# Token sums of two pairs in one set of instructions, 198 pairs by seven products, the last half store on ScalarE's queue, and the first two k tiles in loads of 512 KB

## The chip, the cores and the metric

The kernel runs on one core of a Trainium2 chip (trn2). The metric is the device time of one execution in microseconds (us); a verdict compares medians of several executions of both kernels on the same chip. An instruction belongs to TensorE (PE, with its weight loads PEld), VectorE (DVE), ScalarE (ACT), GpSimd (POOL) or SyncE (SP). SP, POOL and ACT also issue DMA transfers, each through a queue of its own.

## The reference

One layer of a decoder on 256 tokens and 2048 features, in f32, in which nearly all the work is products of the tokens with weight matrices:

```python
h = rmsnorm(x, g_mix[i])
proj = h @ w_in[i]
x_r, g_r, q, k, v, gate_r, gate_a = jnp.split(proj, IN_SPLIT_POINTS, axis=-1)
...
y_r = jax.nn.gelu(g_r) * rg_lru(xc, w_rg_a[i], b_rg_a[i], w_rg_x[i], b_rg_x[i], lru_lambda[i])
y_r = y_r @ w_rnn_out[i]
...
y_a = o.transpose(0, 2, 1, 3).reshape(B, S, D_ATTN) @ w_attn_out[i]
mix = jax.nn.sigmoid(gate_r) * y_r + jax.nn.sigmoid(gate_a) * y_a
x = x + mix @ w_o[i]
h = rmsnorm(x, g_ffn[i])
gu = h @ w_ffn_gu[i]
g, u = jnp.split(gu, 2, axis=-1)
x = x + (jax.nn.silu(g) * u) @ w_ffn_down[i]
ple_gate = jax.nn.sigmoid(rmsnorm(x, g_ple[i]) @ w_ple_gate[i])
x = x + ple_gate * (p[i] @ w_ple_proj[i])
```

## The kernel before

Every f32 operand is split into two parts that TensorE takes in the type float32r: a high part (ACT copies the values into that type) and a low part (DVE subtracts the high part from the values). A product is then three matmuls, high by high, high by low and low by high; `prod` issues them, 128 x 128 of tokens by 128 x 512 of weights each. Names: `raw` and `r` are weights as loaded, `whi`/`wlo` and `shi`/`slo` their parts, `xg`, `hg`, `act`, `mix`, `y`, `ost`, `h3` the split tokens, and `xs`, `hgs`, `as`, `ms`, `ys`, `os`, `h3s` split sums of tokens.

`group` computes the two token tiles (t = 0, 1) by two blocks of 512 columns (A and B), over all k tiles of 128 features. Two k tiles are a pair, and a pair is taken in one of two ways. Plain, it is eight products. By seven products it is a scheme of Strassen's kind over the 2 x 2 token blocks and 2 x 2 weight blocks of the pair: seven products, of which four use sums of weights and four sums of tokens. Two pairs by seven always go together; their weights lie in one tile of 128 x 1024, so that each of the items "11", "21", "22", "T1", "T2", "T3", "T4" is one high part on ACT, one low part on DVE and two products. For T1 to T4 the weights must first be summed: by a DMA of POOL that adds from HBM onto the tile (`pr.add`), or by a `tensor_tensor` of DVE (names `r<-r,r`), which for T1 and T3 needs the block 12 loaded as well (`r12`). The table `how` of `CFG` says, for each group, which of them POOL adds; `xr`, `gu` and the other lists of `CFG` say which pairs go by seven.

The token sums of a pair come from `half_sums`: its 128 x 512 of tokens are four blocks; one DVE instruction of 256 columns and two of 128 make four sums, and `split` makes their high part on ACT and their low part on DVE, 512 columns each.

The first product "T1" of a group is stored in a PSUM bank, from which ACT copies it into a second one ("seeds"), since both blocks need it; the next products that go into the first bank wait for that copy. The copies of PSUM banks by ACT are written `q<-q`, `u<-q`, `pair<-q`, `pair<-u`.

After a group, its results are scaled and gated on ACT and DVE and then turned by TensorE (`pr.turns`, names `gut`, `hgt`, `mxt`, `h3t`, four matmuls of 128 x 128 a pair), before they are the tokens of later groups. These steps are hooks of the group that follows, at the items that `turn` lists.

The order on each engine is no code order: `make` builds all operations, and `schedule` places them by due times with a cost table, under 54 tiles of 128 x 1024 and 8 PSUM banks; `improve` repeats that. So a change of a table moves instructions everywhere. Within an engine and within a queue, order is fixed: an instruction that waits holds back all behind it.

At the start, nine matmuls on zeros (`warm`) keep TensorE busy, and the first k tiles are loaded one by one, 256 KB for each block. At the end, `embed` (`pp`) and the gate give the last output tiles, which SP stores; the last one is stored in two halves.

Of the kernel before, what the change touches and what calls it, by code (L numbers as in the profile page):

```python
# [11 lines left out]
P = 128  # L12
# [79 lines left out]
class Program:  # L92
# [95 lines left out]
    def store(self, dst, i, kb, name="", writes=(), cap=None):  # L188
        return self.op("SP", 0.06, 0.0, lambda nc: nc.sync.dma_start(dst(nc), i.ap()), [i], list(writes), size=kb,
                       name=name, cap=cap)  # L190
# [397 lines left out]
def order_of(ks, nd, lead=0):  # L588
# [24 lines left out]
def build(cfg):  # L613
# [100 lines left out]
    def half_sums(h, name):  # L714


        q = tile("hs", "H")
        a11, a12 = h[:P], h[2 * P:3 * P]
        s3, s1, s2, s4 = (q[c * P:c * P + P] for c in range(4))
        pr.vec(2 * P, lambda nc: nc.vector.tensor_tensor(  # L720
            R3(2)(q[:2 * P].ap()), R3(2)(h[:2 * P].ap()), R3(3)(h[P:].ap())[:, ::2, :], ALU.subtract),
               [h.all], [q[:2 * P]], name="hs")
        tt(s2, s1, a11, ALU.subtract, name="hs")
        tt(s4, a12, s2, ALU.add, name="hs")
        t = split(q.all, name)
        return [(t[c * P:c * P + P], t[512 + c * P:640 + c * P]) for c in (1, 2, 0, 3)]
# [30 lines left out]
    def group(w, cols, ks, pairs, sums, tokens, how, hooks=None, lead=0):  # L757
# [7 lines left out]
        early = {x for x in order if x[0] in "AB"} if lead and nd else ()  # L765
# [13 lines left out]
        for n, x in enumerate(order):  # L779
# [3 lines left out]
            m, dp = x[:2]  # L783
            if m in ("A", "B"):
# [98 lines left out]
    def x_sums(ps):  # L883
        for p in ps:
            if p not in xsum:
                h = tile("h", "H")
                tt(h.all, xg[p][:512].f32(), xg[p][512:].f32(), ALU.add, name="h")
                xsum[p] = half_sums(h, "xs")

    x_sums(xp)  # L890
    for b in range(4):
        for t in range(2):
            q = tile("xq", "H")
            pr.load(q.all, dram("x", (lambda t, b: lambda a: a[t * P:t * P + P, b * 512:b * 512 + 512])(t, b)), 256,
                    name="xq", early=None)
            squares(0, t, b, q.all)
# [34 lines left out]
    xc, xcs, y, ysum, hr = {}, {}, [], {}, {}  # L931

# [54 lines left out]
    def finish(p):  # L987
# [4 lines left out]
        tt(r.all, ps.all, r.all, ALU.mult, name="y")  # L992
        y.append(split(r.all, "y"))
        if p in union("ro"):
            ysum[p] = half_sums(r, "ys")
# [114 lines left out]
    heads, osum = {}, {}  # L1110
    qs, ks_, zst, ost = {}, {}, {}, []
# [95 lines left out]
    def att_o(hp):  # L1207
# [18 lines left out]
        if hp in union("ao"):  # L1226
            h = tile("h", "H")
            act(h.all, ps.all, AF.Copy, name="h")
            ost.append(split(h.all, "ost"))
            osum[hp] = half_sums(h, "os")  # L1230
        else:
            ost.append(split(ps.all, "ost"))
# [54 lines left out]
    mix, msum = {}, {}  # L1287

    def next_mix(p):
        def run():  # L1290
# [6 lines left out]
            if p in union("wo"):  # L1297
                h = tile("h", "H")
                act(h.all, ps.all, AF.Copy, name="h")
                mix[p] = split(h.all, "mix")  # L1300
                msum[p] = half_sums(h, "ms")
# [32 lines left out]
    def next_h(hs, sums, p, gcol, pairs, name):  # L1334
        def run():
            ps = turned(p, name + "t")
            g = pc(gcol, 2 * p, 2)
            if p in pairs:
                h = tile("h", "H")
# [3 lines left out]
                hs[p] = split(h.all, name)  # L1343
                sums[p] = half_sums(h, name + "s")
# [4 lines left out]
    hg, hsum = {}, {}  # L1349
    for g in range(2):  # L1350
# [11 lines left out]
        for p in range(4 * g, 4 * g + 4):  # L1362
            pend.append(next_h(hg, hsum, p, PC_GF, union("gu"), "hg"))
# [4 lines left out]
    h3, sum3 = {}, {}  # L1368
    q_of = [q for q in range(len(FQ)) for _ in range(FQ[q])]
    f0 = [sum(FQ[:q]) for q in range(len(FQ))]  # L1370
    dn_pairs = {p for v in cfg["dn"] for u in v for p in u}

    def gu(g):
# [13 lines left out]
        def turn(f):  # L1387
            def run():
# [4 lines left out]
                if p in dn_pairs:  # L1393
                    h = tile("h", "H")
                    act(h.all, ps.all, AF.Copy, name="h")
                    acts[p] = split(h.all, "act")
                    asum[p] = half_sums(h, "as")
# [6 lines left out]
    def down(q, g):  # L1404
# [19 lines left out]
        if q == len(FQ) - 1:  # L1424
            for p in range(4 * g, 4 * g + 4):
                pend.append(next_h(h3, sum3, p, PC_GP, union("pg"), "h3"))
# [22 lines left out]
    for g in range(2):  # L1449
# [7 lines left out]
        for n in (0, 2, 3, 1) if g else range(4):  # L1457
# [7 lines left out]
            for s in cut:  # L1465
# [3 lines left out]
                    t, 1024 * g + 512 * b, s)), d[s], (s.stop - s.start) // 2, name="out")  # L1469
# [7 lines left out]
CFG = dict(xr=[X2, X2, X4, X4, X4], ro=[F6, F4], gtr=[X4] * 2, v=[X6, X8], qk=[X4, X6, X4, X4], gta=[X4] * 2,  # L1477
           ao=[F4] * 2, wo=[F4, F6], gu=[F4, X8, *[F6] * 9], pg=[F4, X8], dn=[[F4, F6], [[8, 9, 10, 11]] * 2,
           [[16, 17, 18, 19]] * 2], how=dict(xr=[NONE, LATER, SOON, TWO, SOON], gtr=[SOON, ONE], v=[TWO] * 2,
           qk=[SOON, TWO, TWO, ONE], gta=[ALL, LATER], ro=[TWO, ALL], ao=[TWO, SOON], wo=[TWO] * 2, gu=[TWO,  # L1480
           SOON, TWO, LATER, TWO, TWO, TWO, LATER, TWO, TWO, LATER], pg=[ALL, TWO], dn=[ONE, NONE, TWO]),
           lead=8, order=('g1', 'r0', 'r1'), att0=4, every=9, at=(0, 4, 10, 16), turn=[3, 5, 7, 9])
# [5 lines left out]
def make():  # L1488
    pr = build(CFG)
# [79 lines left out]
```

## Time and profile before

| what | value |
|---|---|
| median of 3 runs | 1794.31 us (1792.18 to 1794.45) |
| the profiled execution | 1792.39 us, span 1790.7 us in the profile |
| DMA | 440.54 MB, mean 246 GB/s |
| slowest issue to landing | weights added by POOL, 215 of 512 KB, 8.7 us in the median |
| granted TensorE clock | 0.999 |

A row of the timeline reads: start in us from the span's start, length in us, engine, source line, operation, written tile <- read tiles, sizes, count; in brackets the idle time of the engine before it and what ended that. Lengths of neighbours overlap, so what an instruction costs its engine in a full row is the distance from its start to the next one's.

### The profile page before, as it was taken

How to read it: one execution, taken by the hardware profiler on the slowest of the kernel's cores; microseconds unless marked ns; L12 is line 12 of the kernel's file. 1: busy time of each engine (PE TensorE's matmuls, PEld its weight loads, DVE VectorE, ACT ScalarE, POOL GpSimd, SP SyncE). 2: the span in 40 equal slices, each digit the busy share in tenths (PEclk: the TensorE clock that was granted, in tenths of full speed). 3: DMA queues.
4: the chain of work that ended last, by engine and by line, in shares of the span. 5: the costliest groups of instructions: out<-in, count | busy, mean ns of one | idle time of the engine just before them, and what ended most of it. 6: DMA issues, size and time to landing. Idle time of an engine off the chain costs nothing.

```text
span 1790.7 us, 23886 instructions
## 1 busy us (share of the span) xinstructions
PE 1779.9 (99%) x8295; PEld 1483.2 (83%) x8295; DVE 1675.0 (94%) x1933; ACT 1423.0 (79%) x1962; POOL 202.6 (11%) x239
## 2 busy tenths in 40 slices
PE   9999999999999999999999999999999999999998
PEld 7888888888888888888888888888888788888887
DVE  8999887998799899899999999999999898999989
ACT  8999999876567799999777878677677666778875
POOL 0000000011011100111101011101211001120110
PEclk9999999999999999999999999999999999999999
DMA  9886877769999885888979999988999878999894
GB/s 358 277 223 206 231 224 204 232 181 278 279 253 251 239 219 166 225 231 224 254 233 288 264 272 282 236 250 252 310 262 248 234 216 254 280 264 300 244 282 118
DMA packets 126842, 440.54 MB, mean 246 GB/s; under 512 B 14208, under 2 KB 14848, under 8 KB 126720
## 3 DMA queue, kind: packets, MB, share of 16 engines
q1 hardware_dynamic: 93312, 322.07, 50.4%
q0 software_dynamic: 33264, 116.93, 35.3%
q8 instruction: 65, 1.06, 0.2%
q14 instruction: 57, 0.47, 0.1%
q10 hardware_dynamic: 144, 0.01, 0.0%
HBM read 430.56 MB, written 8.39 MB: 245 GB/s over the span
## 4 chain that ended last, share of the span: by engine, by line
PE 90%; ACT 4%; DMA 2%; DVE 2%; issue 1%; SPq 0%; DVEq 0%; ACTq 0%
PE q L215 55%; PE u L215 29%; PE rg L962 2%; DMA r<-in_w_dram 1%; ACT pair L179 1%; ACT L179 1%; ACT shi L179 1%; DMA raw<-in_w_dram 1%; DVE slo L146 1%; ACT whi L179 1%; PE z L204 1%; PE o L204 1%; PE gut L224 1%; PE e L204 0%; DVE pair L146 0%
## 5 line engine op out<-in xcount | busy, mean ns | idle before, releaser
L146 DVE TENSOR_TENSOR slo<-r,shi 128x1024 fp32r<-128x1024 f32 x686 | 814.3, 1222 | 47.8 <-ACT shi L179 45.1
L179 ACT ACTIVATE shi<-r 128x1024 fp32r<-128x1024 f32 x686 | 701.5, 1055 | 181.6 <-DMA r<-in_w_dram 89.4
L146 DVE TENSOR_TENSOR wlo<-raw,whi 128x1024 fp32r<-128x1024 f32 (+3 forms) x288 | 340.2, 1197 | 19.8 <-ACT whi L179 19.6
L193 POOL DMA_DIRECT2D r<-in_w_dram x215 | 186.6, 870 | 1447.7 <-DVE slo L146 687.7
L179 ACT ACTIVATE whi<-raw 128x1024 fp32r<-128x1024 f32 (+3 forms) x288 | 294.5, 1036 | 20.1 <-DMA raw<-in_w_dram 10.6
L215 PE MATMUL q<-whi,xg 128*128 128x512 f32 x760 | 258.8, 393 | 0.2
L146 DVE TENSOR_TENSOR r<-r,r 128x1024 f32<-128x1024 f32 x177 | 213.7, 1222 | 3.8 <-DMA r<-in_w_dram 3.6
L215 PEld LDWEIGHTS q<-whi,xg 128*128 128x128 f32 x760 | 142.7, 188 | 30.7 <-issue 0.8
L215 PE MATMUL q<-wlo,xg 128*128 128x512 f32 x380 | 148.6, 391 | 0.8 <-DVE wlo L146 0.8
L179 ACT ACTIVATE pair<-u 128x512 f32<-128x512 f32 x85 | 50.6, 595 | 50.8 <-PE u L215 50.0
L215 PE MATMUL q<-whi,hg 128*128 128x512 f32 x264 | 90.6, 391 | 0.0
L215 PE MATMUL q<-shi,hgs 128*128 128x512 f32 x264 | 88.6, 394 | 0.7 <-ACT q L179 0.7
L215 PE MATMUL q<-shi,hg 128*128 128x512 f32 x264 | 88.8, 391 | 0.0
L215 PE MATMUL q<-shi,xs 128*128 128x512 f32 x256 | 88.7, 396 | 0.0
L215 PE MATMUL q<-shi,xg 128*128 128x512 f32 x252 | 86.2, 393 | 0.0
L215 PE MATMUL u<-shi,hgs 128*128 128x512 f32 x264 | 85.9, 390 | 0.0
L215 PE MATMUL u<-shi,xs 128*128 128x512 f32 x256 | 84.7, 391 | 0.0
L215 PEld LDWEIGHTS q<-wlo,xg 128*128 128x128 f32 x380 | 71.5, 188 | 15.7 <-DVE wlo L146 1.9
L215 PE MATMUL u<-whi,xg 128*128 128x512 f32 x200 | 76.0, 391 | 0.0
L215 PE MATMUL q<-whi,act 128*128 128x512 f32 x216 | 73.3, 390 | 0.0
L179 ACT ACT_TABLE_LOAD x52 | 66.7, 1283 | 2.5 <-PEq L1556 1.2
L146 DVE TENSOR_TENSOR pair<-pair,pair 128x128 f32<-128x128 f32 (+1 forms) x156 | 60.6, 413 | 8.4 <-ACT pair L179 7.9
(331 smaller groups left out, 3709.1 us busy)
## 6 DMA issues: line engine op xcount, KB each, us to landing
r<-in_w_dram SPq DMA_DIRECT2D x308, 512.0 KB, 7.4
raw<-in_w_dram SPq DMA_DIRECT2D x262, 512.0 KB, 6.1
r<-in_w_dram POOLq DMA_DIRECT2D x215, 512.0 KB, 8.7
raw<-in_w_dram SPq DMA_DIRECT2D x16, 448.0 KB, 5.0
pair<-in_x_dram SPq DMA_DIRECT2D x16, 256.0 KB, 7.5
kept<-pair POOLq DMA_DIRECT2D x16, 256.0 KB, 8.2
kept<-pair SPq DMA_DIRECT2D x8, 256.0 KB, 5.5
pair<-kept SPq DMA_DIRECT2D x8, 256.0 KB, 6.3
```

Source lines behind the costliest of these rows:

```text
L146: return self.vec(n, lambda nc: nc.vector.tensor_tensor(o.ap(), a.ap(), b.ap(), op), [a, b], [o], name=name, **kw)
L179: nc.scalar.activation(o.ap(), i.ap(), f, **kw)
L193: return self.op("POOL", 0.85, 0.0, lambda nc: nc.gpsimd.dma_start(o.ap(), src(nc), accum_op=ALU.add), list(reads), [o], size=-kb, name=na ...
L204: nc.tensor.matmul(o.ap(), l.ap(), r.ap(), start=start, stop=stop, skip_group_check=True)
L215: nc.tensor.matmul(ps.ap(), x[i].ap(), w[j].ap(), start=a, stop=b, skip_group_check=True)
L224: nc.tensor.transpose(ps[n * P:n * P + P].ap(), s.ap(), ident.ap())
L962: nc.tensor.matmul(ps.ap(), wt[i].ap(), x[j].ap(), start=a and n == 0, stop=b and n == 2, skip_group_check=True) for n, (i, j) in enumerat ...
```

## The change

- `half_sums` takes one or two pairs: `Halves` holds the 128 x 512 of the first pair in one half of a 128 x 1024 tile (`h`) until the second is there, and the four sums of both come from three DVE instructions of 512, 256 and 256 columns, split as 1024 columns once.
- The sums for the first groups are made from x as loaded, scaled by ACT (`x_sums(xp, True)`), not from the split tokens by DVE.
- `CFG`: pairs 2 to 7 instead of 4 to 7 go by seven products in the fourth group of `xr` (198 pairs in all, 196 before); other weight sums go to POOL or DVE; `turn` and `att0` move hooks.
- The first two k tiles are loaded in 512 KB each, columns of A and B together, split in two halves; the number of plain items in front of the first "11" stays 8, of which two now hold both blocks.
- The last half tile is stored by ACT's queue; the first x tiles for the squares may be loaded in two halves, so that the number of transfers is a multiple of eight.

```diff
-    def store(self, dst, i, kb, name="", writes=(), cap=None):
-        return self.op("SP", 0.06, 0.0, lambda nc: nc.sync.dma_start(dst(nc), i.ap()), [i], list(writes), size=kb,
-                       name=name, cap=cap)
+    def store(self, dst, i, kb, name="", writes=(), cap=None, eng="SP"):
+        e = {"SP": "sync", "ACT": "scalar"}[eng]
+        return self.op(eng, 0.06, 0.0, lambda nc: getattr(nc, e).dma_start(dst(nc), i.ap()), [i], list(writes),
+                       size=kb, name=name, cap=cap)
...
-        p[:2] = [(h, k) for k in p[0][1:] for h in "AB"]
+        p[:2] = [("AB", k) for k in p[0][1:]]
...
+    class Halves:
...
+        def done(self, p, h):
+            self.seen.add(p)
+            if not self.both(p):
+                half_sums(h, 1, [p], self.sums, self.name)
+            elif p ^ 1 in self.seen:
+                half_sums(self.tiles.pop(p // 2).all, 2, [p & ~1, p | 1], self.sums, self.name)
+
+    def half_sums(h, n, ps, sums, name):
...
+        q = tile("hs", "L" if n == 2 else "H").all
+        cut = lambda x: x.rearrange("p (g c q) -> p g c q", g=n, c=4)
+        pr.vec(2 * P * n, lambda nc: nc.vector.tensor_tensor(
+            cut(q.ap())[:, :, 0:2], cut(h.ap())[:, :, 0:2], cut(h.ap())[:, :, 1::2], ALU.subtract), [h], [q], name="hs")
+        pr.vec(P * n, lambda nc: nc.vector.tensor_tensor(
+            cut(q.ap())[:, :, 2], cut(q.ap())[:, :, 1], cut(h.ap())[:, :, 0], ALU.subtract), [h, q], [q], name="hs")
+        pr.vec(P * n, lambda nc: nc.vector.tensor_tensor(
+            cut(q.ap())[:, :, 3], cut(h.ap())[:, :, 2], cut(q.ap())[:, :, 2], ALU.add), [h, q], [q], name="hs")
...
+            hi, lo = tile(name, "L", dt=F32R).all, tile(name, "L", dt=F32R).all
+            act(hi, q, AF.Copy, name=name)
+            tt(lo, q, hi.f32(), ALU.subtract, name=name)
...
+            if m == "AB":
+                r = raw_of([(w, x[1], c) for b in cols for c in b])[0]
+                hi, lo = tile("whi", "L", dt=F32R), tile("wlo", "L", dt=F32R)
+                for b in range(2):
+                    s = slice(b * 512, b * 512 + 512)
+                    act(hi[s], r[s], AF.Copy, name="whi")
+                    tt(lo[s], r[s], hi[s].f32(), ALU.subtract, name="wlo")
...
+            if raw:
+                for e in range(2):
+                    s = slice(e * 256, e * 256 + 256)
+                    act(h[s], xt[p][s], AF.Identity, scale=gm[2 * p + e:2 * p + e + 1], name="h")
...
+                         eng="ACT" if s.start else "SP")
...
-CFG = dict(xr=[X2, X2, X4, X4, X4], ro=[F6, F4], gtr=[X4] * 2, v=[X6, X8], qk=[X4, X6, X4, X4], gta=[X4] * 2,
+CFG = dict(xr=[X2, X2, X4, X6, X4], ro=[F6, F4], gtr=[X4] * 2, v=[X6, X8], qk=[X4, X6, X4, X4], gta=[X4] * 2,
...
-           lead=8, order=('g1', 'r0', 'r1'), att0=4, every=9, at=(0, 4, 10, 16), turn=[3, 5, 7, 9])
+           order=('g1', 'r0', 'r1'), att0=3, every=9, at=(0, 4, 10, 16), turn=[3, 4, 5, 6])
```

Three places in the order of instructions bear on the steps of the prediction. The first is DVE's row late in the feed-forward part, between the join of a group's result (`pair<-q,pair`) and the gating `SCALAR_TENSOR_TENSOR` whose results TensorE turns next; `as` are the sums of activations for the group of the down projection that follows. Before:

```order
L146 TENSOR_TENSOR pair_12954<-q_12854,pair_12954 128x512
L720 TENSOR_TENSOR pair_13047<-pair_12126 128x256
L146 TENSOR_TENSOR r_77_12869<-r_77_12869,r_12_12904 128x1024
L146 TENSOR_TENSOR pair_13047<-pair_13047,pair_12126 128x128
L720 TENSOR_TENSOR pair_13047<-pair_12126 128x256
...
L720 TENSOR_TENSOR pair_13047<-pair_12458 128x256
L146 TENSOR_TENSOR pair_12126<-pair_12458,pair_12126 128x128
L146 TENSOR_TENSOR as_13085<-pair_13047,as_13085 128x512
L150 SCALAR_TENSOR_TENSOR pair_12954<-pair_12954,rs_1_9876,pair_12126 128x512
```

The same place in the changed kernel:

```order
L146 TENSOR_TENSOR pair_12912<-q_12801,pair_12912 128x512
L743 TENSOR_TENSOR hs_13006<-h_12401 128x2x256
L146 TENSOR_TENSOR r_78_12822<-r_78_12822,r_21_12862 128x1024
L745 TENSOR_TENSOR hs_13006<-hs_13006,h_12401 128x2x128
L146 TENSOR_TENSOR as_13021<-hs_12962,as_12998 128x1024
L146 TENSOR_TENSOR slo_13031<-r_77_12812,shi_12979 128x1024
L747 TENSOR_TENSOR hs_13006<-h_12401,hs_13006 128x2x128
L150 SCALAR_TENSOR_TENSOR pair_12912<-pair_12912,rs_1_9847,pair_13036 128x512 x2
```

Fourteen instructions stood between the join and the gating, and six do now.

The second place is TensorE where the last product "T1" of a group (weights `shi`/`slo`, tokens `hgs` or `xs`) is followed at once by a product into the same bank. Before, in a gate-and-up group:

```order
L215 MATMUL q_11745<-shi_11779,hgs_9554 128x512
L215 MATMUL q_11745<-slo_11796,hgs_9554 128x512
L215 MATMUL q_11745<-shi_11779,hgs_9554 128x512
L215 MATMUL q_11745<-shi_11743,hgs_9925 128x512
L215 MATMUL q_11745<-slo_11756,hgs_9925 128x512
```

In the changed kernel, in a projection of x:

```order
L216 MATMUL q_2060<-shi_2083,xs_321 128x512
L216 MATMUL q_2060<-slo_2096,xs_321 128x512
L216 MATMUL q_2060<-shi_2083,xs_338 128x512
L216 MATMUL q_2060<-whi_2089,xg_151 128x512
L216 MATMUL q_2060<-wlo_2107,xg_151 128x512
```

Both orders have one such place; at the others, products into another bank stand between.

The third place is SP's queue at the start (`raw` weights, `pair` from `xT` the tokens). Before:

```order
L186 DMA raw_74<-in_w_dram 128x512
L186 DMA pair_70<-in_xT_dram 128x256
L186 DMA raw_79<-in_w_dram 128x512
L186 DMA raw_81<-in_w_dram 128x512
L186 DMA raw_85<-in_w_dram 128x512
L186 DMA pair_70<-in_xT_dram 128x256
L186 DMA raw_88<-in_w_dram 128x1024
```

In the changed kernel:

```order
L186 DMA raw_74<-in_w_dram 128x1024
L186 DMA pair_70<-in_xT_dram 128x256
L186 DMA raw_79<-in_w_dram 128x1024
L186 DMA pair_70<-in_xT_dram 128x256
L186 DMA raw_84<-in_w_dram 128x1024
```

The first four weight loads became two of twice the size; the same bytes are issued ahead of the third tile.

More of the change, by code (lines that the diff above doesn't have):

```diff
@@ L764, in group @@
         q2, q3, q8, U = (psum(n) for n in ("q", "q", "q", "u"))
-        early = {x for x in order if x[0] in "AB"} if lead and nd else ()
+        early = {x for x in order if x[0] in ("A", "B", "AB")} if lead and nd else ()
         q4 = psum("q") if early else U
@@ L1226, in att_o @@
         if hp in union("ao"):
[L1227 to L1230, printed above, removed]
+            h = oh.slot(hp)
+            act(h, ps.all, AF.Copy, name="h")
+            ost.append(split(h, "ost"))
+            oh.done(hp, h)
         else:
@@ L1297, in run @@
             if p in union("wo"):
[L1298 to L1301, printed above, removed]
+                h = mh.slot(p)
+                act(h, ps.all, AF.Copy, name="h")
+                mix[p] = split(h, "mix")
+                mh.done(p, h)
             else:
```

95 lines of the change are left out of this document (58 added, 37 removed).

## The prediction

> **What bounds the kernel now.** I read the page's first part, then the chain of waits, then who TensorE waited for.
>
> ```profile
> PE 1779.9 (99%) x8295; PEld 1483.2 (83%) x8295; DVE 1675.0 (94%) x1933; ACT 1423.0 (79%) x1962; POOL 202.6 (11%) x239
> PE 90%; ACT 4%; DMA 2%; DVE 2%; issue 1%; SPq 0%; DVEq 0%; ACTq 0%
> 523.91 5.44 PE u L215 x24
> ```
>
> TensorE is the bound almost from end to end: 90% of the chain is its own work, and where nothing disturbs it 24 products of 512 columns take 5.44 us, 0.227 us each. Time can come only from fewer matmuls, from the places where TensorE stands still, and from the ends. The timeline of TensorE shows the few places where it stood still for long:
>
> ```profile
> 40.73 0.39 PE L215 MATMUL q<-whi,xg 128*128 128x512 f32 x1
> 41.90 0.50 PE L215 MATMUL q<-wlo,xg 128*128 128x512 f32 x1 [0.78 <-DVE wlo L146]
> ...
> 1273.74 0.39 PE L215 MATMUL q<-shi,hgs 128*128 128x512 f32 x1
> 1274.80 0.51 PE L215 MATMUL q<-shi,hgs 128*128 128x512 f32 x1 [0.67 <-ACT q L179]
> ...
> 1416.52 0.39 PE L215 MATMUL q<-whi,hg 128*128 128x512 f32 x1
> 1417.08 0.50 PE L215 MATMUL u<-whi,hg 128*128 128x512 f32 x1 [0.18 <-ACT pair L179]
> ...
> 1427.91 0.39 PE L215 MATMUL q<-shi,act 128*128 128x512 f32 x1
> 1428.73 0.30 PE L224 MATMUL gut<-ident,pair 128*128 128x128 f32 x1 [0.43 <-DVE pair L150]
> 1429.30 0.55 PE L224 MATMUL gut<-ident,pair 128*128 128x128 f32 x3 [0.27 <-DVE pair L150]
> ```
>
> From start to start, less 0.227 for the product itself (0.11 for a turning matmul), they lose 0.94, 0.83, 0.33, 0.59 and 0.46: 3.15 us in all. That, the ends and the matmul count are the purse.
>
> **Matmuls.** One more couple of pairs goes by seven. In the order of TensorE, 48 plain products' matmuls go and 42 of the seven kind come: 6 fewer, 6 x 0.227 = **-1.36 us**. TensorE is the bound, so this counts whole.
>
> **DVE's account.** The distances from start to start in a full row, and the groups:
>
> ```profile
> 1424.22 1.22 DVE L146 TENSOR_TENSOR slo<-r,shi 128x1024 fp32r<-128x1024 f32 x1
> 1425.35 0.42 DVE L720 TENSOR_TENSOR pair<-pair 128x256 f32<-128x256 f32 x1
> 1425.69 0.29 DVE L146 TENSOR_TENSOR pair<-pair,pair 128x128 f32<-128x128 f32 x1
> 1425.89 0.69 DVE L146 TENSOR_TENSOR as<-pair,as 128x512 fp32r<-128x512 f32 x1
> 1426.49 0.29 DVE L146 TENSOR_TENSOR pair<-pair,pair 128x128 f32<-128x128 f32 x1
> ...
> 1427.83 1.41 DVE L150 SCALAR_TENSOR_TENSOR pair<-pair,rs,pair 128x512 f32<-128x512 f32 x2
> L720 DVE TENSOR_TENSOR pair<-pair 128x256 f32<-128x256 f32 x54 | 21.8, 422 | 0.0
> L146 DVE TENSOR_TENSOR ze<-ze,e 128x256 f32<-128x256 f32 x8 | 3.3, 414 | 0.0
> L1165 DVE TENSOR_TENSOR z<-z,neg 128x256 f32<-128x256 f32 x16 | 6.5, 426 | 2.7 <-PE z L204 2.7
> L146 DVE TENSOR_TENSOR r<-r,r 128x1024 f32<-128x1024 f32 x177 | 213.7, 1222 | 3.8 <-DMA r<-in_w_dram 3.6
> ```
>
> So 1024 columns cost 1.13, 512 cost 0.60, 256 cost 0.34, 128 cost 0.20. A pair's sums were 0.34 + 0.20 + 0.20 + 0.60 = 1.34, two pairs 2.68; at once they are 0.60 + 0.34 + 0.34 + 1.13 = 2.41. The new instructions go over two runs of columns or more; the trace has two runs in the first instruction of the old sums (L720) and in the mask (L1165), 422 and 426 ns against 414 of a plain one of 256 columns, so I take plain prices. If each run cost an instruction's start, 0.07, it would be 81 x 0.07 = 6 us more. 27 times 0.27 is -7.3. Six sums of split tokens leave for ACT: -3.6. Against it the new table has nine more sums of weights on DVE (186 against 177): +10.2, and three more low parts: +3.4. DVE ends at +2.7 of 1675, no term of its own.
>
> [...]
>
> ACT gets twelve scalings, but wider splits: some +6 us, on an engine with 21% idle. POOL adds 210 times in the new order, 5 fewer than in the old; ten more loads of 512 KB on SP and four fewer of 256 KB come with it, 4 MB of 440.
>
> Where the work falls due matters more than its sum. I counted the DVE rows that each stretch of TensorE's order needs and laid these distances on them. For TensorE's 50 to 200 us they rise from 130 to 140 us, for 900 to 1400 they fall from 494 to 492. What DVE did then:
>
> ```profile
> 50.00:200.00 150.00, 139.86 (x196) 1.00 0.81 230
> 900.00:1400.00 500.00, 489.00 (x524) 1.00 0.93 262
> ```
>
> (columns: length, DVE busy, clock, DMA share, GB/s). In the first stretch 10 of 150 us were idle, so 10 more still fit; I take 0. If DVE could not use that idle time, up to 10 us would be late, which the stock built before must cover. In the second the load stays at 98%.
>
> **The early stop (0.94 at 40.73).** DVE was late with a low part. Up to the low part that is tightest there, DVE had 34.1 us of work against 36.3 of products; now the tightest has 35.3 against 39.0: 1.6 us more room than the 0.94 lost, because one more pair of plain k tiles stands ahead of the first "11" and ACT makes the sums. **-0.9**; between 0 (the loads, which come in the same rhythm, are what is late) and -0.9.
>
> **The stop at 1273.74** is the copy of the "T1" bank. The same pattern stands once in the new order, in a projection: **0**, between -0.8 (other products slip between) and +0.8 (a second one).
>
> **The stops at 1416 to 1429 (1.38).** They began with a late load:
>
> ```profile
> 1398.27 13.73 DMA r<-in_w_dram
> r<-in_w_dram SPq DMA_DIRECT2D x308, 512.0 KB, 7.4
> ```
>
> against 7.4 us in the median of SP's loads of `r`. DVE then ran full from the join to the gating at 1427.83: by the rows shown 6.0 us, now 4.7. These 1.3 us cover the 1.05 lost at the turn, if the load comes as late again; where the next late load falls I can't tell. Half of it: **-0.7**, between -1.4 and +1.4 (a second such spot).
>
> **The head.** The first load is twice as long.
>
> ```profile
> 3.74 0.63 ACT L179 ACTIVATE whi<-raw 128x512 fp32r<-128x512 f32 x1 [1.22 <-DMA raw<-in_w_dram]
> 4.40 0.69 DVE L146 TENSOR_TENSOR wlo<-raw,whi 128x512 fp32r<-128x512 f32 x1 [2.79 <-ACT whi L179]
> 5.01 0.48 DVE L150 SCALAR_TENSOR_TENSOR xg<-pair,gm,xg 128x256 fp32r<-128x256 f32 x1
> 4.68 1.05 PE L204 MATMUL warm<-pair,onesr 128*128 128x512 f32 x2
> 5.88 0.47 PE L215 MATMUL q<-whi,xg 128*128 128x512 f32 x1
> ...
> 6.43 0.62 PE L215 MATMUL q<-whi,xg 128*128 128x512 f32 x2
> raw<-in_w_dram SPq DMA_DIRECT2D x262, 512.0 KB, 6.1
> raw<-in_w_dram SPq DMA_DIRECT2D x6, 256.0 KB, 4.6
> ```
>
> The first product follows the end of the warm matmuls (5.73), not the load: the high part was ready at 4.37, the tokens' low part, which the third matmul takes at 6.43, at 5.49. So 0.9 us of delay is hidden. 512 KB took 1.5 longer than 256 KB in the median; with few transfers under way I expect about half. **0**, between -0.3 (block B's weights come along, and k tile 1 in time) and +0.6.
>
> **The tail.** The last additions end DVE's work; SP issues the last stores one by one.
>
> ```profile
> 1785.03 1.35 DVE L146 TENSOR_TENSOR pair<-pair,pair 128x512 f32<-128x512 f32 x3
> 1785.73 1.31 SPq L189 DMA_DIRECT2D out_dram<-pair  x3
> 0.81 0.40 ACTq L186 DMA_DIRECT2D gm<-in_prm_dram  x1
> ```
>
> DVE ends at 1786.38, the last issue at 1787.04. ACT needs 0.40 to issue and holds nothing else then: 1786.38 + 0.03 + 0.40 = 1786.81, **-0.2**. The first half and the whole tiles are now added before it, so the last half may also find emptier DMA engines: to -0.6. Nothing gained if SP's drain waits as long: 0.
>
> [...]
>
> **The sum**: -1.36 - 0.9 - 0.7 - 0.2 = -3.2 us. Made on the profiled execution's own 1792.39 that is 1789.2. This execution stands low among the four times known (1792.18, 1792.39, 1794.31, 1794.45), whose middle is 1793.35; a median of several should fall there, 1 us higher: **1790.2 us**, 0.23% under the median shown.
>
> **The rivals.** About 0.2% (3.6 us) is what a measurement of this kernel tells from no change.
>
> *New stops take the place of the old.* All of the purse but the matmuls and the tail comes back: a late load like that of 1398 elsewhere, a second bank copy. For it: 98% load of DVE late, DMA shares of 0.93. Against it: fewer instructions between join and turn. 1793.35 - 1.6 = 1791.8, no change that can be told.
>
> *The turns now come in a bunch: slower.* `turn` puts four pairs at items 3, 4, 5, 6, not 3, 5, 7, 9. An item is six matmuls, 1.36 us; a turned pair costs DVE 0.60 + 1.20 (half of 2.41), the item's own low part 1.13, together 2.93: 1.57 behind per item, 6.3 after four. Before, two items had 0.60 + 1.34 + 2.26 = 4.20 against 2.72: 1.48 behind per pair, 5.9 after four, but over twice the time, in which the due order could fetch weights ahead. Six groups take four turns each (two each with `mxt`, `hgt`, `h3t`). If the low parts stand less than about 4.8 us ahead there, each loses 1.5 or more: 6 x 1.5 - 3.2 = +5.8, 1799. It decides from that stock downward. For it: the stops at 1428 show DVE without stock. Against it: the sum of work is the same, and the planner may shift turns.
>
> *The pairwise sums are no cheaper*, because instructions over two runs cost more than the mask suggests, or the second pair's turn is awaited too long. Then DVE carries 7 us more, the early and late gains go, the matmuls and the tail stay: 1791.8.
>
> **How the numbers follow.** My forecast 0.58: its own range 1788 to 1792, of which 0.45 lies beyond -0.2% and 0.13 within. New stops 0.20, all within. The bunch 0.15, slower. No cheaper sums 0.07: within 0.05, slower 0.02. So faster 0.45, within 0.38, slower 0.17. The low end is all gains at their bounds (1.4 + 0.9 + 0.8 + 1.4 + 0.3 + 0.6 = 5.4 under 1793.35: 1788), a little lower if a median falls low: 1787.5. The high end takes in a mild bunch, two groups lost, and the bounds of the bank copy: 1795.5.
>
> **What would show it.** Matmuls 8289 in the page. No gap over 0.3 us on TensorE near 40; one gap of 0.8 waiting for ACT in a projection of x, near 200 to 215. The sums' DVE rows: 128x512 at 0.60 and 128x256 at 0.34 from start to start. First product at 5.9. Last issue on ACT some 0.4 after DVE's last add. Wrong: gaps waiting for DVE within 15 us after the groups that take four turns; DVE full and TensorE waiting between 100 and 200 us; more than two loads of over 13 us on the chain.

## The result and the profile after

The changed kernel takes 1786.9 us in the median (7 runs, 1786.16 to 1788.94), the kernel before 1793.27 us (7 runs, 1792.18 to 1794.45). The ratio is 0.9968, with a 95% interval of 0.9957 to 0.9979: 6.4 us faster, where 3.2 were forecast (1790.2 us). The direction was right, the time lies just under the low end of the range (1787.5), and the forecast gain was half of what came.

| what | before | after |
|---|---|---|
| the profiled execution, its span | 1792.39, 1790.7 us | 1786.9, 1785.1 us |
| TensorE's last matmul starts at | 1783.76 | 1780.69 |
| of that, all matmuls at the undisturbed distance | 1771.95 | 1770.59 |
| of that, stops and the start | 11.8 | 10.1 |
| from the last matmul's start to the end | 6.92 | 4.46 |

(the undisturbed distance is the median distance from start to start for each width; the row sums it over all matmuls.) So the span's 5.6 us are 1.36 from the matmuls, 1.7 from stops and 2.5 from the end. Stops of over 0.2 us make up 4.3 us before and 3.9 after, so that only 0.4 of the 1.7 lies in them; the other 1.3 is in delays of under 0.2 us each, whose causes no run here shows. The medians differ by more, 6.4 us, because the profiled execution of before stands 0.9 under its median.

The profile of the changed kernel: its line of busy times, its chain of waits by engine, and then, from the view of whom TensorE waited for (us in all, times, longest), the rows of ScalarE.

```profile
PE 1777.0 (100%) x8289; PEld 1481.6 (83%) x8289; DVE 1677.5 (94%) x1831; ACT 1427.7 (80%) x1951; POOL 198.7 (11%) x234
PE 94%; ACT 2%; DMA 2%; DVE 1%; issue 1%; SPq 0%; DVEq 0%; ACTq 0%
```

```profile
PE u L216 <- ACT pair L179: 1.5, 1, 1.5
PE q L216 <- ACT q L179: 0.7, 1, 0.7
```

8289 matmuls, 102 instructions fewer on VectorE, and its busy time up by 2.5 us, all nearly as worked out. Of the five large stops of before none is left. Two others stand there, on TensorE's timeline:

```profile
209.65 0.39 PE L216 MATMUL q<-shi,xs 128*128 128x512 f32 x1
210.71 0.50 PE L216 MATMUL q<-whi,xg 128*128 128x512 f32 x1 [0.67 <-ACT q L179]
...
417.71 0.39 PE L216 MATMUL q<-whi,y 128*128 128x512 f32 x1
419.57 0.50 PE L216 MATMUL u<-whi,y 128*128 128x512 f32 x1 [1.47 <-ACT pair L179]
```

From start to start, less 0.227, the first loses 0.83: the copy of the "T1" bank in a projection of x, between 200 and 215, as forecast. The second loses 1.63. ScalarE's timeline there:

```profile
417.03 1.06 ACT L179 ACTIVATE whi<-raw 128x1024 fp32r<-128x1024 f32 x1 [2.80 <-DMA raw<-in_w_dram]
417.99 1.04 ACT L179 ACTIVATE shi<-r 128x1024 fp32r<-128x1024 f32 x1
418.94 0.58 ACT L179 ACTIVATE pair<-u 128x512 f32<-128x512 f32 x1
```

ScalarE stood 2.80 us before a high part whose load was late. The copy of bank `u`, for which TensorE was waiting, stood in the same queue behind it and behind one more high part, with its own data there since 417.

The head, in three timelines: ScalarE's first high part, VectorE's low part of the weights and of the tokens, and TensorE.

```profile
4.66 0.63 ACT L179 ACTIVATE whi<-raw 128x512 fp32r<-128x512 f32 x1 [2.13 <-DMA raw<-in_w_dram]
```

```profile
5.33 0.69 DVE L146 TENSOR_TENSOR wlo<-raw,whi 128x512 fp32r<-128x512 f32 x1 [3.71 <-ACT whi L179]
5.94 0.48 DVE L150 SCALAR_TENSOR_TENSOR xg<-pair,gm,xg 128x256 fp32r<-128x256 f32 x1
```

```profile
5.89 0.70 PE L216 MATMUL q<-whi,xg 128*128 128x512 f32 x1
6.42 0.39 PE L216 MATMUL q<-wlo,xg 128*128 128x512 f32 x1
```

The first load came 0.92 us later than before (4.66 against 3.74). The first product still starts at 5.89. The second, which takes the low part that ends at 6.02, starts at 6.42, where 6.12 would be undisturbed and the kernel before has 6.19: 0.3 lost, 0.2 of it new. That the load did it isn't shown: in the run with two sums less (below), whose head is that of the kernel before and whose first high part starts at 3.58, the second product starts at 6.45.

The end holds what the forecast missed. The chain of waits in order of time (start, length, what), first of the kernel before and then of the changed one:

```profile
1762.20 5.45 PE u L215 x24
1767.66 0.02 issue
1767.68 1.21 DVE slo L146
...
1780.77 2.61 DVE pair L146 x5
1783.38 0.38 issue
1783.76 1.94 DVE pair L146 x4
1785.70 0.33 DVEq L1563
1786.04 0.34 DVE pair L146
```

```profile
1774.10 5.44 PE u L216 x24
1779.54 0.73 PE pp L216 x6
...
1780.82 0.77 DVE pair L146 x2
1781.61 0.43 DVE pair L146
```

Before, the chain leaves TensorE at 1767.7: for the last 19 us the end is set by VectorE, which works through its low parts, sums and last additions without a pause (busy for 18.68 of the 18.70 us from 1767.70 to 1786.40). After, the chain stays on TensorE until 1780.3, and VectorE only adds what the last matmuls give. The "DVE 2%" of the chain that the prediction quoted from the page of before holds this stretch; read in order of time it would have told that the last stretch has another bound than the rest.

### The profile page after: what moved, and what is told of

The parts are those of the page before. It is cut to its first block, busy times and chain, and to the rows that moved or that the text cites. A ratio compares the mean times of both kernels' runs of the same rounds, so it can differ in the third digit from the quotient of the medians.

```text
span 1785.1 us, 23773 instructions
## 1 busy us (share of the span) xinstructions
PE 1777.0 (100%) x8289; PEld 1481.6 (83%) x8289; DVE 1677.5 (94%) x1831; ACT 1427.7 (80%) x1951; POOL 198.7 (11%) x234
## 4 chain that ended last, share of the span: by engine, by line
PE 94%; ACT 2%; DMA 2%; DVE 1%; issue 1%; SPq 0%; DVEq 0%; ACTq 0%
PE q L216 57%; PE u L216 30%; PE rg L1013 3%; DMA raw<-in_w_dram 2%; ACT shi L179 1%; PE z L205 1%; PE o L205 1%; PE pp L216 1%; PE gut L225 1%; ACT pair L179 1%; ACT L179 0%; PE e L205 0%; DVE slo L146 0%; PE hdt L225 0%; ACT whi L179 0%
## 5 line engine op out<-in xcount | busy, mean ns | idle before, releaser
L146 DVE TENSOR_TENSOR wlo<-raw,whi 128x1024 fp32r<-128x1024 f32 (+2 forms) x284 | 334.7, 1193 | 27.2 <-ACT whi L179 26.3
L194 POOL DMA_DIRECT2D r<-in_w_dram x210 | 182.6, 871 | 1441.8 <-DVE slo L146 551.3
L179 ACT ACTIVATE whi<-raw 128x1024 fp32r<-128x1024 f32 (+2 forms) x284 | 290.4, 1038 | 30.2 <-DMA raw<-in_w_dram 20.0
L216 PE MATMUL q<-whi,xg 128*128 128x512 f32 x736 | 249.5, 393 | 0.8 <-ACT q L179 0.7
L146 DVE TENSOR_TENSOR r<-r,r 128x1024 f32<-128x1024 f32 x186 | 224.9, 1217 | 0.5 <-DMA r<-in_w_dram 0.4
L216 PEld LDWEIGHTS q<-whi,xg 128*128 128x128 f32 x736 | 138.3, 188 | 30.5 <-ACT q L179 1.7
L216 PE MATMUL q<-wlo,xg 128*128 128x512 f32 x368 | 143.4, 390 | 0.0
L216 PE MATMUL u<-whi,xg 128*128 128x512 f32 x192 | 72.2, 390 | 0.0
L146 DVE TENSOR_TENSOR pair<-q,pair 128x512 f32<-128x512 f32 x89 | 59.0, 682 | 7.1 <-PE q L216 5.2
```

What stands on the lines that cost most here:

```text
L146: return self.vec(n, lambda nc: nc.vector.tensor_tensor(o.ap(), a.ap(), b.ap(), op), [a, b], [o], name=name, **kw)
L179: nc.scalar.activation(o.ap(), i.ap(), f, **kw)
L194: return self.op("POOL", 0.85, 0.0, lambda nc: nc.gpsimd.dma_start(o.ap(), src(nc), accum_op=ALU.add), list(reads), [o], size=-kb, name=na ...
L216: nc.tensor.matmul(ps.ap(), x[i].ap(), w[j].ap(), start=a, stop=b, skip_group_check=True)
```

## The experiments

Every run below was timed in five rounds beside the kernel before, which stood at 1792.55, 1792.82 and 1792.99 us in the three groups of runs. "The constant" is the planner's `SPARE`, by which a transfer's due time is set ahead, 5.0 us in both kernels; where it changes, the same work comes in another order.

### The last half store on SP again

```diff
-                         eng="ACT" if s.start else "SP")
+                         eng="SP")
```

> The changed kernel with its last half store back on SP's queue, all else and the order of every engine the same. Theory (in the changed kernel DVE no longer ends late, so SP has issued the half before at 1781.64 and is free when the last addition ends at 1782.04): 0 to +0.2 us, the span from DVE's last end to the end of the program stays near 3.1 us. Rival (the store from ScalarE is what shortened the tail by 2.5 us): +0.5 to +1.2 us.

Measured: 1786.96 us, ratio 0.9966 (0.9954 to 0.9979), and 4.44 us from the last matmul to the end, against 4.46. In this kernel the store from ScalarE is worth nothing that can be seen; even the 0.2 of the forecast was too much.

### The count of transfers one off

```diff
-    pr = build({**CFG, "cuts": -n % 8})
+    pr = build({**CFG, "cuts": -n % 8 + 1})
```

> The changed kernel with one more early load cut in two, so that the number of transfers is one over a multiple of eight; every engine's compute order is the same. Theory (SP waits at the end for eight semaphores in a fixed order, some 0.06 us each after the last to come; with a multiple of eight the last store's is the last of them): the span from the last store's landing to the end grows by 0.3 to 0.45 us, the whole by as much. Rival (the order of the waits at the end is hidden): 0 within 0.1 us in that stretch.

Measured: 1787.61 us, ratio 0.9975 (0.9966 to 0.9985), 4.82 us at the end: 0.36 longer, as the theory gives. The view of whom SyncE waited for from 1775 on (us in all, times, longest), first in the changed kernel and then here:

```profile
SPq L1622 <- DMA out_dram<-pair: 2.1, 4, 0.7
SPq L1622 <- DMA out_dram<-pair: 2.4, 1, 2.4
```

At the end SyncE takes eight semaphores of transfers one after the other. In the changed kernel the last store's is the last of them, and the step of SyncE that follows them, a drain, starts 0.08 us after that store has landed (1784.24, 1784.33). With the count one off it is the first: seven more follow, 0.06 us apart, and the drain starts 0.51 after the landing (1785.62, 1786.13). From the last landing to the end of the program it is 1.32 us in the four kernels of this document without a multiple of eight (the kernel before among them) and 0.90 to 0.96 in nine of the ten with one. The tenth, with the turned pairs wide apart (below), also starts its drain after 0.08; its 1.26 come from a step of GpSimd behind that. So the count is worth 0.4 us.

The profile of this run, in the order of the changed kernel, shows one more large stop, on TensorE's and ScalarE's timelines:

```profile
1590.07 0.27 PE L225 MATMUL gut<-ident,pair 128*128 128x128 f32 x1
1591.43 0.77 PE L225 MATMUL gut<-ident,pair 128*128 128x128 f32 x5 [1.09 <-DVE pair L150]
```

```profile
1585.46 1.06 ACT L179 ACTIVATE whi<-raw 128x1024 fp32r<-128x1024 f32 x1 [2.74 <-DMA raw<-in_w_dram]
```

A load came late, VectorE's low part waited 1.44 us for the high part, the gating behind it was late, and the turn lost 1.25. That is how the stops of the kernel before at 1416 to 1429 began: the shorter row of VectorE does not cover every such load.

### The two edits at the end alone, on the kernel before

```diff
+                         eng="ACT" if s.start else "SP")
...
+    n = sum(o.size > 0 for o in build(CFG).ops)
+    pr = build({**CFG, "cuts": -n % 8})
```

> The kernel before with the change's two edits at the end alone: the last half store from ScalarE and a number of transfers that is a multiple of eight (some of the x tiles come in two transfers of 128 KB); the compute instructions stand in the order of the kernel before. My theory: the end gains only the 0.35 us of the count, because VectorE still comes to the end full and late (its last low part 3.0 us ahead of the last matmul, in the changed kernel 4.7): from TensorE's last start to the end 6.6 us, time 1792.9 (0.4 under the kernel before). Rival, that these two edits are what took 2.5 us from the end: 4.4 us from the last start to the end, time 1790.8.

Measured: 1794.63 us, ratio 1.0012 (1.0003 to 1.0021); 6.5 us from the last matmul to the end. At the end the theory holds: the two edits alone take 0.5 of 6.9. The count gives 0.4 of it, and issue time 0.2: the last issue, by ScalarE, ends 0.44 us after VectorE (1791.11, 1791.55), where in the kernel before SyncE, still busy with the half before, took 0.66 (1786.38, 1787.04). The landing took 0.1 longer. The time went up all the same. The kernel before needs seven of the x tiles in halves to reach a multiple of eight (the changed one only one). The profiled execution (1796.67, some 2 over the median) shows what may have come of it, on TensorE's and ScalarE's timelines:

```profile
46.12 0.39 PE L216 MATMUL q<-whi,xg 128*128 128x512 f32 x1
48.58 0.50 PE L216 MATMUL u<-shi,xg 128*128 128x512 f32 x1 [2.07 <-ACT pair L179]
```

```profile
46.98 1.06 ACT L179 ACTIVATE whi<-raw 128x1024 fp32r<-128x1024 f32 x1 [2.48 <-DMA raw<-in_w_dram]
```

It is the pattern of 417 again: a load 2.5 us late, and a bank copy queued behind the high part that waits for it. TensorE lost 2.2 us. That the seven more transfers made the load late is the likely cause, not shown by itself.

### The sums pair by pair in the changed kernel

```diff
-            return p ^ 1 in self.pairs
+            return False
```

> The changed kernel with the token sums pair by pair again (three instructions and a split of 512 columns for each), 198 pairs, the same table. DVE gets 81 instructions and 27 low parts more, +7.3 us by the start distances. Theory (lighter sums are what removed DVE's stops and its late end): +1.5 to +4 us, with new waits of TensorE for DVE after the groups whose results are turned, and DVE ending over 2 us after the last matmul. Rival (the gain is the luck of one plan; DVE's sums are hidden): within 1 us either way, DVE's end within 0.5 us of the changed kernel's.

Measured: 1794.55 us, ratio 1.0009 (1.0000 to 1.0018): 7.6 us over the changed kernel, where 1.5 to 4 were expected. VectorE was busy 1685.5 us, 8.0 more for 108 more instructions. TensorE has new stops (1.21 at 46, 1.19 at 855, 0.83 at 862 and 1277 among them), and the end takes 7.2 us. Its chain at the end runs on VectorE:

```profile
1781.79 0.48 issue
1782.27 0.92 DVE slo L146
1783.19 0.22 issue
1783.40 2.34 DVE pair L146 x4
```

Between the two profiles, 2.7 us are the end; the rest is stops. Most of these wait for ScalarE's copies of banks, not for VectorE as expected, and such stops came with another order too. So the next runs change the order alone.

### Other orders for the same work

The changed kernel, the kernel before and the one with sums pair by pair, each with the constant at 4.0; the changed kernel also with 6.0:

```diff
-LOAD_US, ADD_US, SPARE, HORIZON = 1.35 / 512, 2.7 / 512, 5.0, 1000.0
+LOAD_US, ADD_US, SPARE, HORIZON = 1.35 / 512, 2.7 / 512, 4.0, 1000.0
```

> The changed kernel with one constant of its planner moved (the spare time in a transfer's due time 4.0 in place of 5.0): the same work, the same number of instructions on TensorE and DVE, in another order. Theory: TensorE's stops move but sum up within 1 us of the changed kernel's 2.9 us, the time within 1 us. Rival (the luck of one plan is as large as the whole gain): over 2 us slower, or over 1 us faster.

> The kernel before with the planner's spare time of 4.0 us in place of 5.0: the same work in another order. Theory of the orders (each order draws its own few stops, and the changed kernel's with 5.0 is a lucky draw): this kernel moves by 2 us or more either way, between 1789 and 1797, by other stops of 0.8 to 1.4 us on TensorE; then part of the 6.4 us between the two kernels is no property of the edits. Rival, that 5.0 is the better constant for both: 1796 to 1798, slower by about as much (4.7) as the changed kernel was. Rival, that only the changed kernel's order is sensitive: within 1 us of 1793.3.

> The changed kernel with its sums pair by pair (VectorE 8 us longer in all) and the planner's spare time of 4.0 us in place of 5.0. Beside the changed kernel with 4.0 (1791.6) and the two with 5.0 (1794.6 apart, 1786.9 at once) it tells what the sums at once are worth when the order changes too. Theory, that the lighter sums themselves are worth some 3 us and the order the rest: 1793 to 1797, over 1791.6 by 1 to 5. Rival, that only the order counts: 1788 to 1795, on either side of 1791.6. Rival, that the sums at once are worth the whole 7.6: 1799.

> The changed kernel with the planner's spare time of 6.0 us in place of 5.0: the same work in a third order. Theory of the orders: 1787 to 1793, and TensorE's stops are again one to three copies of a bank waited for (0.83 each) and one or two late low parts or loads; the time stands over 1786.9 by what these stops and the end add. Rival, that 4.0 is too short and any longer spare time does: within 1 us of 1786.9.

Measured, in us (ratio to the kernel before, with its interval):

| the constant | kernel before | changed, pair by pair | changed, two pairs at once |
|---|---|---|---|
| 5.0 | 1793.27 | 1794.55 (1.0009, 1.0000 to 1.0018) | 1786.9 (0.9968, 0.9957 to 0.9979) |
| 4.0 | 1796.94 (1.0022, 1.0013 to 1.0031) | 1797.08 (1.0023, 1.0015 to 1.0032) | 1791.64 (0.9996, 0.9987 to 1.0005) |
| 6.0 | not run | not run | 1790.37 (0.9984, 0.9975 to 0.9993) |

An order alone moves the time by 2.5 to 4.7 us; my first theory (within 1 us) fell, and the rival that 5.0 suits all three is not excluded with two or three orders each. Within a row the change keeps its worth: 6.4 us at 5.0 and 5.3 at 4.0, and the sums at once, with the order that comes with them, are worth 7.6 and 5.4, the second more than the 1 to 5 expected. All three orders with the sums at once lie below all four others. So the gain is most likely one of the edits, and not a lucky order, though the order moves it by most of its size. The other parts of the change (198 pairs, the table of weight sums, the sums from x as loaded) were not run alone. The changed kernel with 4.0 differs by 4.8 us of span: 1.1 at the end, 3.7 in stops, most of them bank copies waited for, by the view of whom TensorE waited for:

```profile
PE u L216 <- ACT pair L179: 1.9, 3, 1.2
PE q L216 <- ACT q L179: 1.3, 2, 0.7
PE q L216 <- ACT u L179: 0.7, 1, 0.7
```

### VectorE with more and with less to do near the end

The orders are kept here. In the changed kernel, two low parts are computed twice:

```diff
+    low = [o for o in order if o.eng == "DVE"][-32:-28]
+    for o in low[:2]:
+        o.emit = (lambda f: lambda nc: (f(nc), f(nc)))(o.emit)
```

> The changed kernel, in its own order, with two low parts of 1024 columns, about 25 us before the end, computed twice each: VectorE has 2 x 1.13 = 2.27 us more to do there. Theory, that the end is set by how late VectorE comes to it: it stands idle for 0.46 us among its last additions, so its end moves by some 1.8 and the stretch from TensorE's last start to the end grows from 4.4 to 6.2 us; time 1788.7 (or TensorE stops for a part of it earlier, with the same sum). Rival, that the end hangs on the last matmul and the stores alone and VectorE has the time to spare: 4.4 us from the last start to the end, time within 0.5 of 1786.9.

Measured: 1790.13 us, ratio 0.9984 (0.9975 to 0.9993): 3.2 over the changed kernel, and the span 2.3 longer, for 2.27 us of work. The end takes 5.8 us in place of 4.5, and TensorE stops once for VectorE:

```profile
1764.08 0.39 PE L216 MATMUL pp<-whi,pts 128*128 128x512 f32 x1
1765.17 0.50 PE L216 MATMUL pp<-wlo,pts 128*128 128x512 f32 x1 [0.70 <-DVE wlo L146]
```

1.4 at the end and 0.86 here are 2.2 of the 2.3. Near the end VectorE has no time to spare: what it is given there, the kernel pays whole.

In the kernel before, two sums of weights are left out, so that TensorE multiplies weights as loaded:

```diff
+    for o in [o for o in order if o.eng == "DVE" and o.name == "sum"][-6:-4]:
+        o.emit = lambda nc: None
```

> The kernel before, in its own order, with two sums of weights left out on VectorE some 35 us before the end (TensorE multiplies what was loaded instead of the sums): VectorE has 2.27 us less to do there. Theory, that VectorE's lateness sets the end: from TensorE's last start to the end 4.8 us in place of 6.9 (the floor is the changed kernel's 4.4 and the 0.35 of the count of transfers), time 1791.2. Rival, that it is the store and the waits at the end: 6.9 stays, time 1793.3.

Measured: 1792.94 us, ratio 0.9998 (0.9989 to 1.0007): no change of the time that can be told, and 6.5 us at the end, 0.4 gained and not 2.1. The theory's numbers fell, and the rival's (6.9 and 1793.3) lay nearer. VectorE's timeline shows where the rest went:

```profile
1763.04 1.23 DVE L146 TENSOR_TENSOR slo<-r,shi 128x1024 fp32r<-128x1024 f32 x1 [0.69 <-ACT shi L179]
...
1767.95 1.23 DVE L146 TENSOR_TENSOR slo<-r,shi 128x1024 fp32r<-128x1024 f32 x1 [0.74 <-ACT shi L179]
```

It stood idle for 1.4 us, waiting for high parts that the kernel before, busy until then, never waited for. So in that order less work alone brings VectorE forward by only a part of it: the next wait, ScalarE's high parts, lies close behind.

What all orders have in common shows when the last low part's start on VectorE is set beside the end:

| kernel | last low part before TensorE's last start | last start to end |
|---|---|---|
| changed; store on SP; count off; turns wide; by hand | 5.9 in each | 4.5; 4.4; 4.8; 4.8; 4.4 |
| changed, constant 4.0; 6.0 | 4.9; 4.7 | 5.6; 5.7 |
| changed, two low parts twice | 4.7 | 5.8 |
| before, two sums less | 4.8 | 6.5 |
| before; edits at the end alone | 4.1; 4.1 | 6.9; 6.5 |
| pair by pair, constant 5.0; 4.0 | 3.8; 3.7 | 7.2; 8.0 |
| before, constant 4.0 | 3.2 | 8.2 |

(The rows for the first and the last: 1774.80 and 1780.69; 1783.69 and 1786.84.) The two add up to 10.3 to 11.8 us in all fourteen, while the end itself goes from 4.4 to 8.2: the program ends about that long after VectorE's last low part, wherever TensorE stands. Where no work was added or left out, every kernel with the sums at once has VectorE 4.7 to 5.9 ahead, every other 3.2 to 4.1.

### The narrow turns

```diff
-           order=('g1', 'r0', 'r1'), att0=3, every=9, at=(0, 4, 10, 16), turn=[3, 4, 5, 6])
+           order=('g1', 'r0', 'r1'), att0=3, every=9, at=(0, 4, 10, 16), turn=[3, 5, 7, 9])
```

> The changed kernel with the four turned pairs at items 3, 5, 7 and 9, as before, in place of 3, 4, 5 and 6; nearly the same order elsewhere. My forecast's theory, that the bunch costs nothing because the low parts stand far enough ahead: within 1 us of 1786.9. Rival, that the bunch costs 1.5 us or more in each of the six groups: 1780 or less. A third, that the narrow spacing is worth something: 1788 to 1790, with stops behind the turns.

Measured: 1788.67 us, ratio 0.9976 (0.9965 to 0.9986), 1.8 over the changed kernel, with intervals that overlap. No stop over 0.2 us stands behind the turns in either kernel; the wide one has 0.4 more at 8, 0.4 at 1012 (a bank copy behind a late load, 20 us after the last turn) and 0.4 at the end. So the bunch costs nothing, which was the forecast; that the wide spacing is worse isn't shown.

### Three stops taken away by hand

```diff
-    pr = build({**CFG, "cuts": -n % 8})
-    return pr, improve(pr, ROOM, WINDOW, 20)
+    pr = build({**CFG, "cuts": -n % 8 - 1})
+    order = improve(pr, ROOM, WINDOW, 20)
...
+    def behind(o, p):
+        order.remove(o)
+        order.insert(order.index(p) + 1, o)
...
+    first.emit = half(slice(0, 512))
+    x.emit = (lambda f: lambda nc: (f(nc), half(slice(512, 1024))(nc)))(x.emit)
+    n = {o.n: o for o in order}
+    behind(n[988], n[971])
+    behind(n[972], n[971])
+    for o in (n[1829], n[1835], n[1828], n[1819]):
+        behind(o, n[1818])
```

(`half` loads half of the first tile; the one x tile that came in halves comes whole, so that the count stays a multiple of eight; 988 and 971 are "seven" products, 972 the copy of the "T1" bank, 1819 the copy of bank `u`, 1828, 1829 and 1835 a high part, its low part and another high part.)

> The changed kernel with three stops taken away by hand, the rest of its order kept: the first load comes in two transfers of 256 KB again (and the one x tile in two transfers whole, so that the count stays a multiple of eight); near 209 the copy of the T1 bank goes ahead on ScalarE's queue and one product of another bank stands behind it; near 417 the bank copy goes ahead of the high part that waits for a late load. Theory, that every stop of TensorE counts whole: -0.3 at the head (second product at 6.12 in place of 6.42), -0.7 near 209, -1.6 near 417, together 2.6 under the changed kernel: 1784.3, with the same 4.4 us at the end. Rival, that what is won comes back in a later wait (VectorE is full and TensorE then comes earlier to its low parts): the three rows gain, but the time stays within 1 of 1786.9, with new stops waiting for VectorE or a longer end.

Measured: 1788.23 us, ratio 0.9970 (0.9959 to 0.9982). All three rows gained, on TensorE's timeline:

```profile
6.20 0.40 PE L216 MATMUL q<-wlo,xg 128*128 128x512 f32 x1
...
210.04 0.39 PE L216 MATMUL q<-shi,xg 128*128 128x512 f32 x1
210.42 0.50 PE L216 MATMUL q<-whi,xg 128*128 128x512 f32 x1
...
418.70 0.39 PE L216 MATMUL q<-whi,y 128*128 128x512 f32 x1
418.92 0.39 PE L216 MATMUL u<-whi,y 128*128 128x512 f32 x1
```

The second product starts at 6.20, near 209 only 0.15 is lost, near 418 nothing: 2.5 us won. The kernel is no faster than the changed one; the view of whom TensorE waited for shows why:

```profile
PE rg L1013 <- DVE wlo L146: 1.4, 1, 1.4
PE u L216 <- DVE slo L146: 0.6, 2, 0.4
```

The copy that went ahead near 209 put ScalarE's next scalings back (their first from 209.15 to 210.28), VectorE's convolution waited for them, and the low part that follows it came 1.1 later, while TensorE came 0.3 earlier: 1.5 us lost at 217. Another 0.6 was lost at 427 and 0.5 at 1023. So the rival's mechanism was right, though its number (within 1 of 1786.9) was missed by 0.3. Neither this kernel nor any other of these runs beats the changed one.

## Why the prediction was right in sign and half in size

**Matmuls, -1.36.** 8289 and -1.36, as worked out.

**VectorE's account, "+2.7, no term of its own".** The account was right (1675.0 to 1677.5 us of busy time), and so were its prices. The groups of the new sums, and rows that follow one another on VectorE's timeline:

```profile
L743 DVE TENSOR_TENSOR hs<-h 128x512 f32<-128x512 f32 x27 | 18.4, 682 | 1.0 <-PE u L216 0.7 <-ACT h L179 0.4
L745 DVE TENSOR_TENSOR hs<-hs,h 128x256 f32<-128x256 f32 x27 | 11.2, 416 | 0.1
```

```profile
1736.20 0.68 DVE L146 TENSOR_TENSOR pair<-pp,pair 128x512 f32<-128x512 f32 x1
1736.80 0.41 DVE L747 TENSOR_TENSOR hs<-h,hs 128x256 f32<-128x256 f32 x1
1737.13 0.68 DVE L146 TENSOR_TENSOR pair<-pair,pair 128x512 f32<-128x512 f32 x1
```

A sum of 256 columns over several runs costs 0.33 from start to start, as long (416 ns) as a plain one (414 in the kernel before); the rival of sums that are no cheaper fell. By the run with the sums pair by pair, an instruction fewer was worth 8.0 / 108 = 0.074 us, the 0.07 of the forecast.

The conclusion failed: **"no term of its own" is the step that was wrong**, and with it the tail. The forecast looked at VectorE's stock at 50 to 200 and at 900 to 1400 us, and never at the last 50, where VectorE of the kernel before runs almost without a pause (busy for 50.44 of 51.40 us from 1735 to 1786.4), comes late, and sets the end. There an instruction added cost its time, as the low parts computed twice show (in the changed kernel, 2.27 us of work for 2.3 us of span). That one saved always gains it isn't so: two sums less gave 0.4 of 2.27.

**The tail, -0.2 (to -0.6): -2.5.** This is the mis-sized term. It was worked out from the last store alone, which brought nothing here (4.46 against 4.44 us with SyncE). What came instead, by the traces' times: VectorE ends 1.35 us after the last matmul's start and not 2.62; the last issue ends 0.44 after that and not 0.67; the last store lands 1.76 after its issue and not 2.32; and from there to the end it is 0.90 and not 1.32. These are 1.3, 0.2, 0.6 and 0.4 us, and the last is the count of transfers, for which the forecast had no term. The landing is as quick from SyncE's queue (1.83) and takes 2.2 to 2.9 in every kernel here whose VectorE ends later than 1.35 after the last matmul, so it goes with VectorE's end and not with the queue. That lateness of VectorE sets the end is shown by the low parts computed twice; that the sums at once are what made it earlier rests on the seven orders (three with the sums at once, two pair by pair, two of the kernel before), which all fall on the right side, and is not shown beyond that.

What the store from ScalarE saved is issue time: with the edits at the end alone the issue took 0.44 us in place of 0.66, the 0.2 of the forecast, and the landing 0.1 longer; in the changed kernel, where SyncE was free by then, not even that (0.44 from ScalarE, 0.36 from SyncE).

**The stops, -0.9, 0, -0.7 and 0 for the head: -1.6; measured -1.7.** That the sum came out is luck. The stops over 0.2 us, which the forecast was about, gave only 0.4; the rest came from delays of under 0.2 us, for which it had no term. Of its parts: the stop at 40.73 is gone, with two small ones in its place (0.2 at 46, 0.3 at 51). The copy of the "T1" bank stands where the order put it. The stops at 1416 to 1429 are gone whole in this execution, but one of the kind came back at 1590 in the run with the count one off, with 1.25. The next late load, whose place "I can't tell", is that of 417, with 1.6, which the forecast's bounds allowed for and its sum did not. The head lost 0.3, inside its bounds, 0.2 more than before: of the 1.5 us that a load of 512 KB took longer in the median, 0.92 came about, on a cover of 0.9 for the first product. Whether the second was late for that is open.

**The rivals.** New stops took the place of most of the old in this order (of the large ones 3.15 us before, 2.46 after), so this rival had the mechanism, and the time escaped it by the end and the small delays; in the two others of the same kernel (13.8 and 13.4 us of stops and start, against 10.1 and the 11.8 of before) they came whole and more. The bunch of turns didn't show.

## What to carry to other kernels

Read the chain of waits in order of time at the end of the program by itself: an engine that is not the bound over the whole span can set the end, and work added there can count whole (here 2.27 us on VectorE made the span 2.3 longer). Where a planner makes the order, compare an edit under two or three of its orders before a few us are put down to it. And look in an in-order queue for short copies, on which the bound engine waits, behind work that waits for a load: that was the largest stop of the changed kernel and of three others here (1.3 to 2.2 us), but moving copies ahead by hand won their stops without making the kernel faster.

## What the runs showed that was not expected

The spread between orders of the same work (1786.9 to 1791.6 us for three orders) is three quarters of the whole effect of the change. Taking 2.27 us from a full VectorE gave back 1.4 at once as waiting for ScalarE, while adding the same amount cost all of it. And cutting seven early transfers of 256 KB into halves, with nothing else changed before the end, went together with a load that came 2.5 us late and a stop of 2.2 us.
